# 1/rms of layer B's rows read from PSUM, their low parts on VectorE, and later weights' sums and scaling queued behind the rows

## Chip, cores and metric

The kernel runs on 1 core of one Trainium2 chip. The metric is the device time in microseconds (us) of one execution. The engines are TensorE (PE; its weight loads are PEld), VectorE (DVE), ScalarE (ACT), GpSimd (POOL) and SyncE (SP), which issues the DMAs. All engines work through their own queue in order.

## What is computed

A decoder trunk of two layers on 1024 tokens of width 1024. Layer A is a gated short convolution, layer B a stick-breaking attention with 16 heads of 64. What concerns the change is the seam between them: x1, the output of layer A, is normalised by its rms, and scaled and shifted with vectors worked out from c, before it is projected to keys, values, queries and the gate z.

```python
def rmsnorm(x, g):
    y = xf * lax.rsqrt(jnp.mean(xf * xf, axis=-1, keepdims=True) + EPS)
    return (y * g).astype(x.dtype)

def modulated_norm(x, g, shift, scale):
    return rmsnorm(x, g) * (1.0 + scale[:, None, :]) + shift[:, None, :]
...
# layer A ends with x1 = x + gate * (y @ w_out); then, for layer B:
hkv = modulated_norm(x, kv_norm_g, kv_shift, kv_scale)
k_flat, v_flat = jnp.split(hkv @ w_kv, 2, axis=-1)
h = modulated_norm(x, norm_g, shift, scale)
q, z = jnp.split(h @ w_qz, 2, axis=-1)
o = stick_breaking_attention(split_heads(q), k, v)
return x + gate * ((o * jax.nn.silu(z)) @ w_out)
```

## The kernel before

Activations lie transposed: the 1024 features are 8 tiles of 128 partitions (index kt or j), the 1024 tokens run along the free axis, cut into two halves of 512 columns. Each product of float32 numbers is made of three TensorE passes: both factors are split into a high part (a copy by ACT, rounded) and a low part (the difference), and high x high, high x low and low x high are summed in PSUM (lines 180 to 182 in `linear`). `split` makes the two parts: line 142 the high part on ACT, line 143 the low part on the engine that it is given. Weights go through the same `split` (whi, wlo), with POOL for the low part.

Layer B's gain is multiplied into the weights, not into the rows: `scaled` (line 158) multiplies a tile of weights by the gain, and `shift_terms` (lines 163 and 165: one start and seven sums on DVE) collects what the shift contributes; `shift_bias` makes a bias column of it. So the rows themselves need only 1/rms.

The stage of the change is the loop over the two halves near line 416. For each output tile j of layer A: weights are loaded and split, the row tile xr of xT is loaded into an s buffer (10 of them), TensorE sums 24 matmuls, DVE adds the gated result to xr (line 426, "the sum" in this text), SP writes it to x1_dram, ACT squares it (429, 432) and DVE adds up the squares (433). After eight tiles `rms_scale` sums the squares over features by transposing on TensorE and reducing on DVE (90, 91), works out 1/rms in twelve small DVE steps (197 to 204), broadcasts it to all partitions with four transpositions (210, "the row block"), and copies it from PSUM to an SBUF tile, rbc (217). DVE multiplies the eight rows by rbc (436), ACT makes x1h, and POOL makes x1l; in the second half every other x1l is made by DVE.

TensorE goes on with the second half's output tiles (s_3418 to s_3682 in the listings, j = 0 to 7) while the first half's rows are finished, and with keys and queries of the first half (`project_qkv(0)`) while the second half's are. Then come values, attention of head pair 0 (`attention`: scores L589 and L590, sigmoid L594, scan L598, transposition L608, the parts ah L611 and al L612, sums L622 and L623), the z projection of pair 0 (`silu_z`), and the projections of pair 1. Their weights come through `load_weights` with a gain, so `scaled` is called for each of them.

The order of each engine's queue is set when the program is built, by a scheduler that goes by its own estimate of the times; `tc.high_priority()` puts a block's instructions ahead where they could stand in several places. PSUM has four tags (mm, z, tr, o) of two banks each.

Of the kernel before, what the change touches and what calls it, by code (L numbers as in the profile page):

```python
# [9 lines left out]
F32 = mybir.dt.float32  # L10
F32R = mybir.dt.float32r
AF = mybir.ActivationFunctionType
ALU = mybir.AluOpType
AX = mybir.AxisListType.X

P = 128
D = 1024
T = 1024
KT = D // P
HALF = 512  # L20
# [17 lines left out]
def decoder_kernel(ctx, tc, vecs, xT, a_mod, kv_mod, b_mod, w_in, w_out_a, w_kv, w_qz, w_out_b, outT):  # L38
    nc = tc.nc
    PSUM = bass.MemoryType.PSUM  # L40

    const = ctx.enter_context(tc.tile_pool(name="const", bufs=1))
# [4 lines left out]

    PS_BUFS = {"mm": 2, "z": 2, "tr": 2, "o": 2}
    seq = [0]

    def ps_tile(tag):
        return psum.tile([P, HALF], F32, name=f"ps_{tag}", tag=tag, bufs=PS_BUFS[tag])

    def ps_any():
        tags = ("mm", "z", "tr")
        seq[0] += 1
        return ps_tile(tags[seq[0] % len(tags)])
# [36 lines left out]
    def column_sums(out, src):  # L94
        for _ in sum_groups(out, src):
            pass
# [44 lines left out]
    def split(hi, lo, full, lo_eng):  # L141
        nc.scalar.activation(hi, full, AF.Copy)  # L142
        lo_eng.tensor_tensor(lo, full, hi.bitcast(F32), op=ALU.subtract)  # L143


    def load_weights(src, gain=None, hi_tag="whi", lo_tag="wlo", pool=None, bufs=2, stage=None, shift=None):
        raw = (stage or raw_tile)()
        nc.sync.dma_start(raw, src)
        hi = (pool or wpool).tile([P, KT * P], F32R, name="whi", tag=hi_tag, bufs=bufs)
        lo = (pool or wpool).tile([P, KT * P], F32R, name="wlo", tag=lo_tag, bufs=bufs)  # L150
        terms = raw if gain is None else scaled(raw, gain, shift)
        split(hi, lo, raw, nc.gpsimd)
        return terms, hi, lo

    def scaled(raw, gain, shift):
        terms = shift_terms(raw, shift)
        raw3 = raw.rearrange("p (k n) -> p k n", k=KT)
        nc.vector.tensor_tensor(raw3, raw3, gain.unsqueeze(2).broadcast_to([P, KT, P]), op=ALU.mult)
        return terms

    def shift_terms(raw, shift):
        acc = const.tile([P, P], F32, name="bacc", tag="bacc", bufs=3)
        nc.vector.tensor_scalar(acc, raw[:, 0:P], shift[:, 0:1], None, op0=ALU.mult)
        for kt in range(1, KT):
            nc.vector.scalar_tensor_tensor(  # L165
                acc, raw[:, kt * P:(kt + 1) * P], shift[:, kt:kt + 1], acc, op0=ALU.mult, op1=ALU.add)
        return acc
# [17 lines left out]
    def rms_columns(ssq, lo_t=0, hi_t=T, more=None, total=None):  # L185
        n = (hi_t - lo_t) // P
        v = const.tile([P, 8], F32, name="rv", tag="rv", bufs=2)[:, :n]
        y = const.tile([P, 8], F32, name="ry", tag="ry", bufs=2)[:, :n]
        t = const.tile([P, 8], F32, name="rt", tag="rt", bufs=2)[:, :n]
        if total is not None:  # L190
            pass
        elif more is None:
            column_sums(v, ssq[:, lo_t:hi_t])
            total = v
        else:
            total = column_totals([(ssq[:, lo_t:hi_t], one), (more, one)], n)
        nc.vector.tensor_scalar(v, total, 1.0 / D, EPS, op0=ALU.mult, op1=ALU.add)
        I32 = mybir.dt.int32
        nc.vector.tensor_scalar(t.bitcast(I32), v.bitcast(I32), 1, None, op0=ALU.arith_shift_right)
        nc.vector.tensor_scalar(y.bitcast(I32), t.bitcast(I32), -1.0, float(0x5F3759DF), op0=ALU.mult, op1=ALU.add)  # L200
        for _ in range(3):
            nc.vector.tensor_mul(t, y, y)
            nc.vector.scalar_tensor_tensor(t, t, -0.5, v, op0=ALU.mult, op1=ALU.mult)
            nc.vector.scalar_tensor_tensor(y, t, 1.5, y, op0=ALU.add, op1=ALU.mult)
        return y

    def row_block(y, c0, w):
        pb = ps_tile("o")
        for i in range(w):
            nc.tensor.transpose(pb[:, i * P:(i + 1) * P], y[:, c0 + i:c0 + i + 1].broadcast_to([P, P]), ident)  # L210
        return pb[:, :w * P]
# [7 lines left out]
    def rms_scale(ssq, rbc, lo_t=0, hi_t=T):  # L219
        rms_rows(rms_columns(ssq, lo_t, hi_t), rbc, lo_t, hi_t)  # L220

    def halves():
        return [slice(h * HALF, (h + 1) * HALF) for h in range(NH)]
# [4 lines left out]
    tmp = papw.enter_context(tc.tile_pool(name="tmpa", bufs=1))  # L228

    def stile():  # L230
        return tmp.tile([P, HALF], F32, name="s", tag="s", bufs=10)

    rbc_a = const.tile([P, T], F32, name="rbc", tag="rbc", bufs=1)
    def ytile():
# [94 lines left out]
    with tc.high_priority():  # L329
        for sl in halves():  # L330
            for kt in range(KT):
                x = stile()
# [37 lines left out]
    for j in range(KT):  # L370
# [37 lines left out]
        if 2 <= j < 2 + len(PARTS):  # L408
            name, w, part, bcol, gcol = PARTS[j - 2]
            mods[name] = mod_vec(w, part, bcol, name, gain_col=gcol)  # L410


    rbc_b = const.tile([P, T], F32, name="rbc", tag="rbc", bufs=1)
    x1h = [xk.tile([P, T], F32R, name="x1h", tag="xk") for _ in range(KT)]
    x1l = [xk.tile([P, T], F32R, name="x1l", tag="xk") for _ in range(KT)]
    for sl in halves():
        ssq1 = tmp.tile([P, HALF], F32, name="ssq1", tag="graw", bufs=3)
        xs = []
        for j in range(KT):
            w = load_weights(w_out_a[j])[1:]  # L420
            xr = stile()
            xs.append(xr)
            nc.sync.dma_start(xr, xT[j * P:(j + 1) * P, sl])
            ps = ps_any()
            linear(ps, w, yh, yl, sl)
            nc.vector.scalar_tensor_tensor(xr, ps, mods["gate_a"][:, j:j + 1], xr, op0=ALU.mult, op1=ALU.add)
            nc.sync.dma_start(x1_dram[j, :, sl], xr)
            if j == 0:
                nc.scalar.activation(ssq1, xr, AF.Square)
            else:  # L430
                sq = tmp.tile([P, HALF], F32, name="sq1", tag="graw", bufs=3)
                nc.scalar.activation(sq, xr, AF.Square)
                nc.vector.tensor_add(ssq1, ssq1, sq)
        rms_scale(ssq1, rbc_b[:, sl], 0, HALF)
        for kt, x in enumerate(xs):
            nc.vector.tensor_mul(x, x, rbc_b[:, sl])
            split(x1h[kt][:, sl], x1l[kt][:, sl], x, nc.vector if sl.start and kt % 2 else nc.gpsimd)
        if sl.start == 0:

            def first_raw(raw, w, m):  # L440
                nc.sync.dma_start(raw, w)
                return raw, scaled(raw, mods["gain_" + m], mods["shift_" + m])

            firsts = [
                first_raw(tmp.tile([P, D], F32, name="raw1", tag="gacc", bufs=1), w_kv[0], "kv"),
                first_raw(tmp.tile([P, 2 + T], F32, name="raw1", tag="v", bufs=2)[:, :T], w_qz[0], "b"),
                first_raw(raw_tile(), w_kv[NPAIR], "kv")]
# [299 lines left out]
    for c, (a, b) in enumerate(CHUNKS):  # L747
        sl = slice(a, b)
        for j in range(EARLY, KT):
# [4 lines left out]
            sq = squares(j, sl, c == len(CHUNKS) - 1 and j == KT - 1)  # L754
# [45 lines left out]
```

## Time and profile before

| | us |
|---|---|
| median of 3 runs (lowest, highest) | 1213.46 (1213.27, 1217.39) |
| the profiled execution | 1214.38 |
| its span in the trace, first to last instruction | 1212.6 |
| PE busy | 1162.2 (96%) |
| PEld busy | 983.3 (81%) |
| DVE busy | 883.2 (73%) |
| ACT busy | 456.9 (38%) |
| POOL busy | 369.3 (30%) |

[...] Matmuls overlap, so one of 512 columns shows a duration of 0.39 us and starts every 0.23 us at the full clock; at half of it 0.63 and 0.43. Rows of the timeline give start and duration in us, engine, line, operation, output tile and inputs, the shape, the count of like instructions that are merged in the row, and in square brackets how long the engine sat idle before it and what ended that.

### The profile page before, as it was taken

To read this page: it belongs to the slowest core of one execution; us is meant where nothing else is said; L and a number is where in the kernel's file an instruction comes from. 1 tells how busy PE (TensorE), PEld (TensorE's weight loads), DVE (VectorE), ACT (ScalarE), POOL (GpSimd) and SP (SyncE) were. 2 spreads that over 40 slices of the span, in tenths; PEclk is the share of its full clock that TensorE was granted. 3 is DMA by queue.
4 is the path that set the end of the run, shared out by engine and by line. 5 is a ranking of instruction groups with operands and counts; after the bars stand their busy time and mean duration, and the time that the engine had idled before them with its cause. 6 is when DMAs were issued, how large, how long until landed. Compare 5 with 4: busy or idle time off the path is not lost.

```text
span 1212.6 us, 15743 instructions
## 1 busy us (share of the span) xinstructions
PE 1162.2 (96%) x5920; PEld 983.3 (81%) x5920; DVE 883.2 (73%) x1297; ACT 456.9 (38%) x750; POOL 369.3 (30%) x217
## 2 busy tenths in 40 slices
PE   7996999999999999879999999999999999999995
PEld 6884888888888888658888888888888888887885
DVE  7589841355445478676989888889988889677466
ACT  4324322111211233323455454454445445454341
POOL 3020544333423546532031231312223031221324
PEclk9797999999999999879999999999999999999997
DMA  9454431154354543413422313232232322553103
GB/s 373 175 167 147 159 101 52 51 175 147 119 182 151 168 139 137 148 39 91 101 66 61 105 53 83 66 89 77 68 84 72 94 68 61 156 206 125 56 16 138
DMA packets 61435, 138.45 MB, mean 114 GB/s; under 512 B 7472, under 2 KB 11696, under 8 KB 61360
## 3 DMA queue, kind: packets, MB, share of 16 engines
q1 hardware_dynamic: 61360, 137.46, 35.7%
q8 instruction: 46, 0.75, 0.3%
q14 instruction: 29, 0.24, 0.1%
HBM read 103.87 MB, written 14.68 MB: 98 GB/s over the span
## 4 chain that ended last, share of the span: by engine, by line
PE 78%; DVE 16%; issue 3%; ACT 1%; POOL 1%; DMA 1%; DVEq 0%; SPq 0%; POOLq 0%; ACTq 0%
PE ps_mm L180 11%; PE ps_mm L181 11%; PE ps_mm L182 11%; PE ps_tr L180 5%; PE ps_tr L181 5%; PE ps_tr L182 5%; PE ps_z L181 5%; PE ps_z L182 4%; PE ps_z L180 4%; PE ps_tr L608 4%; DVE sfx L598 4%; DVE bacc L165 3%; PE ps_o L623 3%; PE ps_o L622 2%; PE ps_z L590 2%
## 5 line engine op out<-in xcount | busy, mean ns | idle before, releaser
L143 POOL TENSOR_TENSOR wlo<-raw,whi 128x1024 fp32r<-128x1024 f32 x87 | 218.7, 2516 | 612.5 <-ACT whi L142 513.8
L598 DVE TENSOR_TENSOR_SCAN sfx<-sfx,floor 128x128 f32<-128x128 f32 (+2 forms) x192 | 221.1, 1171 | 17.2 <-ACT sfx L594 17.2
L181 PE MATMUL ps_mm<-x1l,whi 128*128 128x512 f32 x480 | 190.5, 397 | 4.4 <-DVE x1l L143 3.9
L180 PE MATMUL ps_mm<-x1h,whi 128*128 128x512 f32 x480 | 192.1, 400 | 2.6 <-ACT x1h L142 2.2
L182 PE MATMUL ps_mm<-x1h,wlo 128*128 128x512 f32 x480 | 188.5, 393 | 0.0
L142 ACT ACTIVATE whi<-raw 128x1024 fp32r<-128x1024 f32 x87 | 92.1, 1058 | 166.0 <-issue 60.1
L611 ACT ACTIVATE ah<-ps_tr,minus 128x512 fp32r<-128x512 f32 (+1 forms) x160 | 100.3, 645 | 108.2 <-PE ps_tr L608 106.7
L612 DVE SCALAR_TENSOR_TENSOR al<-ps_tr,ah 128x512 fp32r<-128x512 f32 (+1 forms) x160 | 97.3, 623 | 42.7 <-ACT ah L611 42.2
L594 ACT ACTIVATE sfx<-ps_z 128x128 f32<-128x128 f32 (+2 forms) x192 | 90.6, 491 | 81.6 <-PE ps_z L590 80.6
L181 PEld LDWEIGHTS ps_mm<-x1l,whi 128*128 128x128 f32 x480 | 90.8, 189 | 22.0 <-DVE x1l L143 4.6
L180 PEld LDWEIGHTS ps_mm<-x1h,whi 128*128 128x128 f32 x480 | 90.7, 189 | 20.6 <-ACT x1h L142 2.4
L182 PEld LDWEIGHTS ps_mm<-x1h,wlo 128*128 128x128 f32 x480 | 90.8, 189 | 17.7
L120 DVE SCALAR_TENSOR_TENSOR gacc<-graw,cs,gacc 128x512 f32<-128x512 f32 x84 | 71.2, 863 | 37.2 <-DMA graw<-b_mod 23.5
L623 PE MATMUL ps_o<-al,vv 128*128 128x256 f32 x320 | 83.2, 295 | 5.1 <-DVE al L612 5.0
L608 PE MATMUL ps_tr<-ident,sfx 128*128 128x128 f32 x576 | 87.2, 274 | 0.0
L622 PE MATMUL ps_o<-ah,vv 128*128 128x256 f32 x320 | 85.7, 281 | 0.1
L623 PEld LDWEIGHTS ps_o<-al,vv 128*128 128x128 f32 x320 | 60.4, 189 | 13.3 <-DVE al L612 10.1
L589 PE MATMUL ps_z<-kh,qq 128*128 128x128 f32 (+1 forms) x192 | 69.1, 365 | 0.7 <-ACT sfx L594 0.7
L622 PEld LDWEIGHTS ps_o<-ah,vv 128*128 128x128 f32 x320 | 60.5, 189 | 7.4 <-ACT ah L611 0.6
L608 PEld LDWEIGHTS ps_tr<-ident,sfx 128*128 128x128 f32 x576 | 65.4, 141 | 1.0
L590 PE MATMUL ps_z<-kl,qq 128*128 128x128 f32 (+1 forms) x192 | 65.4, 349 | 0.0
L181 PE MATMUL ps_mm<-nl,whi 128*128 128x512 f32 x152 | 59.8, 393 | 2.7 <-DVE nl L324 2.7
(280 smaller groups left out, 2482.2 us busy)
## 6 DMA issues: line engine op xcount, KB each, us to landing
raw<-w_in SPq DMA_DIRECT2D x29, 512.0 KB, 3.9
graw<-b_mod SPq DMA_DIRECT2D x48, 256.0 KB, 3.1
stage<-a_mod SPq DMA_DIRECT2D x16, 512.0 KB, 8.7
s<-xT SPq DMA_DIRECT2D x32, 256.0 KB, 4.5
graw<-kv_mod SPq DMA_DIRECT2D x32, 256.0 KB, 3.3
raw<-w_qz SPq DMA_DIRECT2D x16, 512.0 KB, 4.0
raw<-w_out_a SPq DMA_DIRECT2D x16, 512.0 KB, 3.6
raw<-w_kv SPq DMA_DIRECT2D x16, 512.0 KB, 3.6
```

Of the source, the lines that this page charges most:

```text
L142: nc.scalar.activation(hi, full, AF.Copy)
L143: lo_eng.tensor_tensor(lo, full, hi.bitcast(F32), op=ALU.subtract)
L180: nc.tensor.matmul(ps, lhsT=wh, rhs=ah[kt][:, sl], start=(kt == kts[0]), stop=False)
L181: nc.tensor.matmul(ps, lhsT=wh, rhs=al[kt][:, sl], start=False, stop=False)
L182: nc.tensor.matmul(ps, lhsT=wl, rhs=ah[kt][:, sl], start=False, stop=(kt == kts[-1]))
L594: nc.scalar.activation(om, zps[:, :w], AF.Sigmoid, scale=-SC)
L598: nc.vector.tensor_tensor_scan(rev, rev, floor[:, z0:z0 + w][:, ::-1], sf[r][:, s0 + w:s0 + w + 1], op0=ALU.mult, op1=ALU.max)
L608: nc.tensor.transpose(tp[:, s * P:(s + 1) * P], rows[r][:, jb * P - c0:(jb + 1) * P - c0], ident)
L611: nc.scalar.activation(ah[:, :w], tp[:, :w], AF.Identity, bias=minus)
L612: nc.vector.scalar_tensor_tensor(al[:, :w], tp[:, :w], -1.0, ah[:, :w].bitcast(F32), op0=ALU.add, op1=ALU.subtract)
L622: nc.tensor.matmul(ops[:, cols], lhsT=vs, rhs=ah[:, rs], start=first, stop=False)
L623: nc.tensor.matmul(ops[:, cols], lhsT=vs, rhs=al[:, rs], start=False, stop=end)
```

## The change

The column sums of the squares are made by matmuls with one column (a path that `rms_columns` had, and the kernel's last chunk used): the running sum of seven squares and the eighth square go in apart, so the last addition on DVE and the reduce fall away. 1/rms is not copied to SBUF: the multiplications read the row block in PSUM. All low parts x1l are made by DVE. The block stands under `tc.high_priority()`. Weights with a gain call `scaled` under `tc.issue_after(...)`: in the order these instructions stand behind the last x1l made so far; for pair 0's z weights and all later ones that is the last row of the second half. The s buffers become 11.

```diff
@@ load_weights @@
-        terms = raw if gain is None else scaled(raw, gain, shift)
+        if gain is None:
+            terms = raw
+        else:
+            with tc.issue_after(last["x1"].ins):
+                terms = scaled(raw, gain, shift)
         split(hi, lo, raw, nc.gpsimd)
@@ stile @@
-        return tmp.tile([P, HALF], F32, name="s", tag="s", bufs=10)
+        return tmp.tile([P, HALF], F32, name="s", tag="s", bufs=11)
@@ the loop over halves @@
-    rbc_b = const.tile([P, T], F32, name="rbc", tag="rbc", bufs=1)
...
                 nc.scalar.activation(sq, xr, AF.Square)
-                nc.vector.tensor_add(ssq1, ssq1, sq)
-        rms_scale(ssq1, rbc_b[:, sl], 0, HALF)
-        for kt, x in enumerate(xs):
-            nc.vector.tensor_mul(x, x, rbc_b[:, sl])
-            split(x1h[kt][:, sl], x1l[kt][:, sl], x, nc.vector if sl.start and kt % 2 else nc.gpsimd)
+                if j < KT - 1:
+                    nc.vector.tensor_add(ssq1, ssq1, sq)
+        with tc.high_priority():
+
+            scale = row_block(rms_columns(ssq1, 0, HALF, sq), 0, 4)
+            for kt, x in enumerate(xs):
+                nc.vector.tensor_mul(x, x, scale)
+                nc.scalar.activation(x1h[kt][:, sl], x, AF.Copy)
+                last["x1"] = nc.vector.tensor_tensor(x1l[kt][:, sl], x, x1h[kt][:, sl].bitcast(F32), op=ALU.subtract)
```

Three places of the queues. In the listings of the changed kernel lines are 4 to 8 higher: the sum is L430, the addition of squares L438, the multiplication L443, x1l on DVE L445, `scaled` L163, `shift_terms` L168 and L170.

DVE, the first half's rows, between the sums of the second half's tiles j=1 and j=2; before:

```order
L426 SCALAR_TENSOR_TENSOR s<-ps_tr,gate_a,s 128x512
L433 TENSOR_TENSOR ssq_3411<-ssq_3411,sq_3483 128x512
L217 COPY rbc<-ps_o 128x512
L436 TENSOR_TENSOR s<-s,rbc 128x512 x8
L426 SCALAR_TENSOR_TENSOR s<-ps_mm,gate_a,s 128x512
```

DVE at the same place in the changed kernel:

```order
L430 SCALAR_TENSOR_TENSOR s<-ps_tr,gate_a,s 128x512
L443 TENSOR_TENSOR s<-s,ps_o 128x512 x8
L438 TENSOR_TENSOR ssq_3411<-ssq_3411,sq_3483 128x512
L445 TENSOR_TENSOR x1l<-s,x1h 128x512 x5
L430 SCALAR_TENSOR_TENSOR s<-ps_mm,gate_a,s 128x512
L445 TENSOR_TENSOR x1l<-s,x1h 128x512 x3
L430 SCALAR_TENSOR_TENSOR s<-ps_z,gate_a,s 128x512
```

The copy is gone, and five low parts stand ahead of the sum of j=2 and three more ahead of that of j=3. The low part of tile 0, which frees the buffer that j=3's row is loaded to, was POOL's before.

TensorE, where the second half's tile j=5 (ps_mm_3608, weights whi_3602) begins; before:

```order
L180 MATMUL ps_mm_3608<-yh_664,whi_3602 128x512
L181 MATMUL ps_mm_3608<-yl_665,whi_3602 128x512
L180 MATMUL ps_z_3646<-yh_664,whi_3640 128x512
L181 MATMUL ps_z_3646<-yl_665,whi_3640 128x512
L182 MATMUL ps_mm_3608<-yh_664,wlo_3603 128x512
L180 MATMUL ps_mm_3608<-yh_820,whi_3602 128x512
```

And in the changed kernel:

```order
L185 MATMUL ps_mm_3608<-yh_664,whi_3602 128x512
L186 MATMUL ps_mm_3608<-yl_665,whi_3602 128x512
L187 MATMUL ps_mm_3608<-yh_664,wlo_3603 128x512
L185 MATMUL ps_mm_3608<-yh_820,whi_3602 128x512
L186 MATMUL ps_mm_3608<-yl_821,whi_3602 128x512
```

The two matmuls of tile j=6 (ps_z_3646) now stand behind the whole of j=5. In the same queue the row block of the first half stands 12 matmuls earlier than before, behind two matmuls of j=2; that of the second half stands where it stood, behind the first half's queries, with the totals' one-column matmuls after 22 of the 48 matmuls of the first half's keys and queries.

DVE, the second half's 1/rms, from the last sum on; before (the start):

```order
L426 SCALAR_TENSOR_TENSOR s<-ps_tr,gate_a,s 128x512
L173 TENSOR_REDUCE bias<-ps_mm 128x1
L163 TENSOR_SCALAR bacc<-raw,shift_b 128x128
L165 SCALAR_TENSOR_TENSOR bacc<-raw,shift_b,bacc 128x128
L433 TENSOR_TENSOR ssq_3411<-ssq_3411,sq_3711 128x512
L165 SCALAR_TENSOR_TENSOR bacc<-raw,shift_b,bacc 128x128 x6
L158 TENSOR_TENSOR raw<-raw,gain_b 128x1024
L173 TENSOR_REDUCE bias<-ps_mm 128x1
L163 TENSOR_SCALAR bacc<-raw,shift_kv 128x128
L91 TENSOR_REDUCE rv<-ps_o 128x4
```

And in the changed kernel the end of the same stretch:

```order
L209 SCALAR_TENSOR_TENSOR ry<-rt,ry 128x4
L178 TENSOR_REDUCE bias<-ps_mm 128x1
L443 TENSOR_TENSOR s<-s,ps_o 128x512 x8
L178 TENSOR_REDUCE bias<-ps_mm 128x1
L445 TENSOR_TENSOR x1l<-s,x1h 128x512 x8
L168 TENSOR_SCALAR bacc<-raw,shift_b 128x128
L168 TENSOR_SCALAR bacc<-raw,shift_kv 128x128
```

The sums and scalings of two weights (bacc and raw) have moved from among the steps of 1/rms to behind the last low part, where they are dealt between the evacuations of keys and queries. The x1h of a row waits for its multiplication alone, each x1l for all eight.

## Rows read from the trace of the kernel before

**Rows 1.** Windows: us; PE, PEld, DVE, ACT, POOL busy; PEclk; DMA share; GB/s.

```profile
485.50:495.70 10.20, 4.81 (x12) 3.43 (x12) 6.63 (x6) 4.83 (x7) 9.87 (x6) 0.67 0.76 241
495.70:509.60 13.90, 13.90 (x62) 11.46 (x61) 6.44 (x5) 3.39 (x4) 4.82 (x2) 1.00 0.35 126
521.50:540.10 18.60, 9.97 (x25) 6.83 (x26) 17.66 (x27) 7.03 (x11) 9.42 (x6) 0.63 0.07 15
```

**Rows 2.** Timeline of TensorE, first hole: tile j=5 (ps_mm) and j=6 (ps_z).

```profile
487.80 0.50 PE L180 MATMUL ps_mm<-yh,whi 128*128 128x512 f32 x1 [2.20 <-ACT whi L142]
...
491.73 0.79 PE L180 MATMUL ps_z<-yh,whi 128*128 128x512 f32 x1 [3.20 <-ACT whi L142]
```

**Rows 3.** Timeline of ACT in the first hole.

```profile
485.65 0.63 ACT L432 ACTIVATE sq<-s 128x512 f32<-128x512 f32 x1 [3.45 <-DVE s L426]
...
486.71 1.04 ACT L142 ACTIVATE whi<-raw 128x1024 fp32r<-128x1024 f32 x1
...
490.64 1.04 ACT L142 ACTIVATE whi<-raw 128x1024 fp32r<-128x1024 f32 x1
```

**Rows 4.** Timeline of DVE ahead of the first hole.

```profile
473.40 11.56 DVE L436 TENSOR_TENSOR s<-s,rbc 128x512 f32<-128x512 f32 x8
484.88 0.74 DVE L426 SCALAR_TENSOR_TENSOR s<-ps_mm,gate_a,s 128x512 f32<-128x512 f32 x1
```

**Rows 5.** Timeline of POOL, same stretch.

```profile
479.23 9.81 POOL L143 TENSOR_TENSOR x1l<-s,x1h 128x512 fp32r<-128x512 f32 x6
489.00 2.35 POOL L143 TENSOR_TENSOR wlo<-raw,whi 128x1024 fp32r<-128x1024 f32 x1
```

**Rows 6.** Timeline of DVE, from the stage's last sum to the second half's rows.

```profile
509.86 0.75 DVE L426 SCALAR_TENSOR_TENSOR s<-ps_tr,gate_a,s 128x512 f32<-128x512 f32 x1 [1.55 <-PE ps_tr L182]
...
517.85 0.69 DVE L91 TENSOR_REDUCE rv<-ps_o 128x4 f32<-128x512 f32 x1
...
521.21 1.23 DVE L158 TENSOR_TENSOR raw<-raw,gain_kv 128x1024 f32<-128x1024 f32 x1
...
524.90 8.18 DVE L436 TENSOR_TENSOR s<-s,rbc 128x512 f32<-128x512 f32 x8
```

**Rows 7.** Timeline of TensorE, second hole and the z projection of pair 0.

```profile
521.22 0.27 PE L172 MATMUL ps_mm<-ident,bacc 128*128 128x128 f32 x1
523.51 0.62 PE L210 MATMUL ps_o<-ident,ry 128*128 128x128 f32 x4 [2.02 <-DVE ry L204]
526.31 0.71 PE L180 MATMUL ps_mm<-x1h,whi 128*128 128x512 f32 x1 [2.17 <-ACT x1h L142]
...
534.81 0.80 PE L181 MATMUL ps_mm<-x1l,whi 128*128 128x512 f32 x1 [3.90 <-DVE x1l L143]
...
552.20 0.45 PE L180 MATMUL ps_mm<-x1h,whi 128*128 128x512 f32 x1
```

**Rows 8.** Groups by line and shape, DVE, 440 to 545 us: count, busy us, mean ns.

```profile
L436 DVE TENSOR_TENSOR s<-s,rbc 128x512 f32<-128x512 f32 x16 | 19.7, 1304 | 0.1
...
L143 DVE TENSOR_TENSOR x1l<-s,x1h 128x512 fp32r<-128x512 f32 x4 | 5.8, 1502 | 0.0
...
L165 DVE SCALAR_TENSOR_TENSOR bacc<-raw,shift_kv,bacc 128x128 f32<-128x128 f32 x14 | 4.9, 351 | 0.2
```

**Rows 9.** The same view from 70 to 545 us: layer A's multiplications by 1/rms.

```profile
L353 DVE TENSOR_TENSOR s<-s,rbc 128x512 f32<-128x512 f32 x4 | 2.7, 685 | 0.0
...
L353 DVE TENSOR_TENSOR s<-ps_tr,rbc 128x512 f32<-128x512 f32 x2 | 1.4, 678 | 0.0
```

**Rows 10.** Timeline of DVE, end of the kernel: 1/rms of the last 256 columns.

```profile
1202.31 0.16 DVE L197 TENSOR_SCALAR rv<-ps_o 128x2 f32<-128x2 f32 x1 [1.55 <-PE ps_o L104]
...
1206.30 2.74 DVE L743 TENSOR_TENSOR out<-x,ps_o 128x256 f32<-128x256 f32 x8 [0.84 <-PE ps_o L210]
```

**Rows 11.** The page's DMA issues: KB each, median us to landing.

```profile
s<-xT SPq DMA_DIRECT2D x32, 256.0 KB, 4.5
```

**Rows 12.** The page's costliest groups: the scan of the attention.

```profile
L598 DVE TENSOR_TENSOR_SCAN sfx<-sfx,floor 128x128 f32<-128x128 f32 (+2 forms) x192 | 221.1, 1171 | 17.2 <-ACT sfx L594 17.2
```

More of the change, by code (lines that the diff above doesn't have):

```diff
@@ L49, in decoder_kernel @@
     seq = [0]
+    last = {}
     def ps_tile(tag):
```

## The prediction

> **What bounds the kernel now.** I read the windows of the stage around the change first, since the share of busy time over the whole span (TensorE 96%) hides where TensorE is not fed. Between 462 and 560 us there are two holes [rows 1]: from 485.5 to 495.7 TensorE works 4.81 of 10.2 us at a granted clock of 0.67, and from 521.5 to 540.1 it works 9.97 of 18.6 us at 0.63. Between them it is never idle (13.90 of 13.90). So an edit here pays only by what it takes out of these two holes, and whatever VectorE (DVE) saves elsewhere is worth nothing.
>
> *First hole.* TensorE's own rows name what it waits for: 2.20 us, then 3.20 us, each for a ScalarE (ACT) copy of weights, whi [rows 2]. ACT's rows show why these are late: the first copy, at 486.71, stands behind the square that starts at 485.65, and the second, at 490.64, again behind a square [rows 3]. A square waits for its sum on DVE (L426), and the sum of tile j=2, at 484.88, stands behind eight multiplications of rows by 1/rms that take 11.56 us [rows 4]. GpSimd (POOL) is late too: six low parts x1l in one piece until 489.0, and only then the low part of the same weights, which ends at 491.35 [rows 5]; the third matmul of tile j=5 needs it. The next sum (j=3) waited for its xT tile, whose buffer such a low part frees.
>
> *Second hole.* DVE's rows: the last sum of the stage starts at 509.86 (A below), but the reduce that begins 1/rms starts at 517.85, since shift sums and scalings of later weights are dealt in between (the one at 521.21 is 1.23 us, ahead of steps that the chain still needs); then the copy of 1/rms to SBUF, and at 524.90 the multiplications, 8.18 [rows 6]. TensorE finishes its cover at 521.49, waits 2.02 us for the last step of 1/rms, 2.17 for the first x1h, and 3.90 for a low part that DVE writes only after all eight multiplications [rows 7].
>
> **The change part by part.**
>
> *Multiplications read PSUM.* The 16 of before have two SBUF inputs and take 1304 ns in the mean [rows 8]. The nearest rows with a PSUM input and the same 512 columns are L353's: 678 ns, and 685 where both inputs are in SBUF and none was stopped [rows 9]. So the place of the operand costs nothing by itself; what falls away is the waiting for POOL. I take 0.61 us from start to start (L743, 8 of 256 columns in 2.74 us [rows 10], is 0.34 each, the same plus its fixed part): 4.9 us for eight. The two copies go. L353's two rows put PSUM 7 ns lower, so I charge nothing for it. [...]
>
> *Low parts on DVE.* 16 instead of 4; POOL loses 12. DVE's four took 1502 ns in the mean [rows 8]. Alone they should take what L353's SBUF form takes, 685 ns [rows 9], 0.61 start to start. Low bound 0.61, high 1.50. In the first half POOL now has only one weights' part per 5.4 us of TensorE (2.35 us each [rows 5]), so DVE is stopped once, not eight times: I take 0.61 and one stop of 2.4 us per half.
>
> *First hole, worked.* 1/rms is sent out on TensorE 12 matmuls earlier (its place in the queue, told with the change), some 2.7 us at 0.224 us a matmul (13.90 us for 62 [rows 1]), and the copy is gone, so the rows start near 470.3 instead of 473.4. Eight at 0.61 end at 475.2; one square's addition; five low parts with one stop for POOL's 2.4 us: 481.2; the sum of j=2 then, against 484.88. Its square ends by 482.6, the weights' copy of j=5 (1.04 us as in [rows 3]) by 483.7, its low part on POOL, whose x1l are gone, by 486.2. TensorE reaches j=5 at 485.5 plus 0.5 for the eight one-column matmuls that replace four transpositions, and its third matmul 0.45 later: no wait, or one below 0.3 us. The two matmuls of j=6 that stood third and fourth in j=5's block, and waited for the second copy, have moved behind it. The load of j=3's row is issued when the first low part is done (about 479) and lands 4.5 later [rows 11], ahead of its sum. So the 24.1 us from 485.5 to 509.6 shrink to 74 matmuls (12 and 62 in the windows) at 0.224 = 16.6: 7.5 less 0.5, **7.0 us**. Low bound: low parts at 1.50 each put the sum of j=2 at 484.9 as before, TensorE again waits 2.2 us and POOL's gain alone is left, 2 us. High bound 7.5.
>
> *Second hole, worked, from A.* TensorE's 48 matmuls of cover end at A+11.6 plus 0.5 for the added ones, and the row block now follows in its queue without waiting, if 1/rms is ready. The same chain at the kernel's end takes 3.99 us from totals to the first PSUM multiplication [rows 10]; the totals stand 22 matmuls into the cover, near A+6, so it is ready at A+10, with the later weights' steps out of its way. The queue of TensorE, not DVE, decides: multiplications at A+12.9 (before A+15.0). They end at A+17.8; the first low part, behind one small reduce, at A+18.6, and TensorE runs from A+18.7 without a stop. Before, it ran from 534.81, A+24.95, with eight of the half's 48 matmuls done, in the changed queue two: 6 more, 1.36 us at the full clock. I leave the slow stretch after resuming as long as it was (534.8 to 540.1), as TensorE is idle about as long. 24.95 - 18.7 - 1.36 = **4.9 us**. With low parts at 1.50 DVE still feeds TensorE, which takes six matmuls per low part, only the first is 0.9 later: low bound 4.0; high 5.5 with a shorter slow stretch.
>
> *Later weights' sums and scaling behind the rows.* Two sets: 14 sums at 351 ns [rows 8], two starts, two scalings at 1.23 [rows 6], some 8 us. They lay in front of the rows; now they follow the last low part (A+25.1), dealt among the evacuations of keys and queries, and the first set ends near A+32. Cover: the z projection of head pair 0, at 552.20 (A+42.3) [rows 7], 4.9 earlier A+37.4. Its weights need 1.04 on ACT [rows 3] and 2.4 on POOL after the scaling: A+35.5. Cost nothing, margin 1.9 us; past it each microsecond counts fully.
>
> *Square sums by one-column matmuls, an 11th s buffer.* The last addition and two reduces fall off DVE, in the cover. The extra buffer moves one xT load and with it DVE's order near 84 to 112 us, where DVE is full. Following the rows there, TensorE has three matmuls more behind it at the same time: a gain of 0.7, or a loss of as much; I take 0.
>
> **Sum.** 7.0 + 4.9 = 11.9 us from the profiled execution's 1214.38: 1202.5. The median shown lies 0.9 below that execution; between the two I say **1202**.
>
> **Rivals.**
>
> *A, the low parts on DVE are stopped by POOL throughout.* A DVE operation with two SBUF inputs takes 1304 to 1502 ns where POOL works beside it, and 685 where it was not stopped [rows 8, 9]; the low parts keep two SBUF inputs. If each takes 1.50, the first hole gives 2 and the second 4: 1208.4. For it: the four of before ran beside a single weights' part and still took 1502. Against: that mean holds one long stop, and POOL's queue is nearly empty now. [...]
>
> *B, nothing to speak of: the order of the first two head pairs gives it back.* The order of DVE and TensorE differs through head pairs 0 and 1 as well, where DVE is nearly full. If the attention there loses 6 to 10 us, 1209 to 1213. For it: a long list of swaps of scans and al. Against: many put al earlier, which is what TensorE waits for.
>
> *C, slower.* The same mechanism with a larger price: an al behind a scan, 1171 ns [rows 12], stops TensorE. The gain is used up when ten of the some 40 al of two pairs are so delayed, and the kernel is slower by over 0.5% from 16 on (18 us): 1221 at 16.
>
> **How the numbers follow.** Forecast (both holes shrink, gain 9 to 14): 0.66. A: 0.16, of which about half is still over 0.5%. B: 0.12. C: 0.06. 0.5% is 6.1 us, about what a measurement of this kernel can tell from none. Faster 0.66 + 0.08 + a little of B = 0.78; same 0.16; slower 0.06. The range takes the high bounds (7.5 + 5.5 + 0.7, so 1200) with a microsecond over, and on the other side A: 1199 to 1209, leaving out B's far half and C.
>
> **What would show it.** Right: multiplications at 0.6 to 0.75 us each; TensorE's wait for whi before j=5 below 0.5 us and its clock at full until the second hole; the second hole's row block without a wait; one wait of about 4 us for x1h and x1l; no wait for the z weights of pair 0; POOL without x1l. Wrong: a low part over 1 us in the mean, a wait for wlo of j=5, al waits in pairs 0 and 1, or a longer slow stretch in the second hole.

## The result, and the profile after

The changed kernel takes 1199.51 us in the median (1197.34 to 1202.63) against 1214.26 for the kernel before, measured beside it: a ratio of 0.9887, 95% interval 0.9857 to 0.9918. Forecast were 1202, 1199 to 1209. Run a second time (`changed_again` below) it took 1201.68, a ratio of 0.9901 (0.9875 to 0.9927).

The windows of the changed kernel, with the columns of [rows 1]:

```profile
460.00:480.00 20.00, 20.00 (x94) 16.63 (x94) 17.98 (x31) 10.06 (x15) 7.79 (x3) 1.00 0.41 135
480.00:500.00 20.00, 20.00 (x90) 16.51 (x89) 13.85 (x12) 6.50 (x9) 9.61 (x4) 1.00 0.57 183
...
512.50:521.50 9.00, 4.62 (x15) 3.11 (x14) 8.60 (x15) 6.91 (x11) 1.29 (x1) 0.81 0.01 2
```

The first hole is gone: TensorE is busy without a break at the full clock (1.00) from 460 to 500 (and on to 512.5: 12.50 of 12.50 us, at 1.00). Of the second, 9 us are left, in which it works 4.62.

DVE of the changed kernel, where [rows 4] and [rows 6] show the kernel before:

```profile
467.55 4.87 DVE L443 TENSOR_TENSOR s<-s,ps_o 128x512 f32<-128x512 f32 x8
...
472.95 5.29 DVE L445 TENSOR_TENSOR x1l<-s,x1h 128x512 fp32r<-128x512 f32 x5
478.16 0.74 DVE L430 SCALAR_TENSOR_TENSOR s<-ps_mm,gate_a,s 128x512 f32<-128x512 f32 x1
478.82 1.88 DVE L445 TENSOR_TENSOR x1l<-s,x1h 128x512 fp32r<-128x512 f32 x3
...
508.76 0.16 DVE L209 SCALAR_TENSOR_TENSOR ry<-rt,ry 128x4 f32<-128x4 f32 x1
512.76 0.29 DVE L178 TENSOR_REDUCE bias<-ps_mm 128x1 f32<-128x128 f32 x1 [3.83 <-PE ps_mm L177]
513.19 4.87 DVE L443 TENSOR_TENSOR s<-s,ps_o 128x512 f32<-128x512 f32 x8
517.98 0.28 DVE L178 TENSOR_REDUCE bias<-ps_mm 128x1 f32<-128x128 f32 x1
518.18 7.11 DVE L445 TENSOR_TENSOR x1l<-s,x1h 128x512 fp32r<-128x512 f32 x8
```

Eight multiplications take 4.87 us, not 11.56 and 8.18. The low parts take 5.29 and 1.88 in the first half, 7.11 in the second. The last step of 1/rms is at 508.76, and DVE then sits idle for 3.83 us until TensorE comes to the bias and the row block, which stand next to each other in its queue.

ACT and POOL of the changed kernel, the two parts of the weights of j=5:

```profile
479.47 1.05 ACT L143 ACTIVATE whi<-raw 128x1024 fp32r<-128x1024 f32 x1
```

```profile
480.59 2.41 POOL L144 TENSOR_TENSOR wlo<-raw,whi 128x1024 fp32r<-128x1024 f32 x1 [4.11 <-ACT whi L143]
```

TensorE of the changed kernel at the second hole, for [rows 7]; the first row is one of the two batches of one-column matmuls that make the totals:

```profile
505.59 0.95 PE L105 MATMUL ps_o<-one,sq 128*128 128x1 f32 x8
...
512.55 0.60 PE L215 MATMUL ps_o<-ident,ry 128*128 128x128 f32 x4
...
514.60 0.50 PE L185 MATMUL ps_z<-x1h,whi 128*128 128x512 f32 x1 [1.17 <-ACT x1h L444]
...
518.32 0.80 PE L185 MATMUL ps_mm<-x1h,whi 128*128 128x512 f32 x1 [3.22 <-DVE bias L178]
518.92 0.80 PE L186 MATMUL ps_mm<-x1l,whi 128*128 128x512 f32 x1
```

The row block no longer waits. The long wait that is left is put down to a bias: the reduce at 517.98 stands behind the eight multiplications and holds a PSUM bank that the keys need. The first x1l, at 518.18, comes 0.2 us later still, and the matmul that takes it starts at 518.92 without a wait of its own; mending the bias alone would have gained little.

**Where the time went.** Three rows cut the span into stretches that can be compared between runs: the transposition of gacc on TensorE near 235 us (gacc is transposed several times; this one makes shift_kv), the stage's last sum on DVE (A), and the last gating product on POOL (G). Of the kernel before, A being in [rows 6]:

```profile
235.20 1.03 PE L90 MATMUL ps_o<-ident,gacc 128*128 128x128 f32 x8
...
1130.30 1.29 POOL L644 TENSOR_TENSOR o<-o,sgb 128x512 f32<-128x512 f32 x1
```

Of the changed kernel's second profile, `changed_again`:

```profile
233.86 1.03 PE L91 MATMUL ps_o<-ident,gacc 128*128 128x128 f32 x8
...
502.06 0.75 DVE L430 SCALAR_TENSOR_TENSOR s<-ps_tr,gate_a,s 128x512 f32<-128x512 f32 x1 [1.48 <-PE ps_tr L187]
...
1117.10 1.29 POOL L652 TENSOR_TENSOR o<-o,sgb 128x512 f32<-128x512 f32 x1
```

The differences of such rows, for all kernels of this study (us, one profile each; the median is that of all runs):

| kernel | to gacc | gacc to A | A to G | G to end | median |
|---|---|---|---|---|---|
| before | 235.20 | 274.66 | 620.44 | 82.3 | 1214.26 |
| changed | 231.59 | 268.18 | 613.45 | 82.4 | 1199.51 |
| changed_again | 233.86 | 268.20 | 615.04 | 82.4 | 1201.68 |
| s_buffers_10 | 230.24 | 268.20 | 615.41 | 82.6 | 1199.73 |
| no_deferral | 234.92 | 268.20 | 615.64 | 82.5 | 1200.32 |
| xl_on_pool | 231.67 | 270.90 | 615.55 | 82.6 | 1203.24 |
| rbc_in_sbuf | 228.55 | 269.61 | 615.83 | 82.5 | 1202.91 |
| before_11_buffers | 235.85 | 273.04 | 620.53 | 82.4 | 1210.91 |
| psum_operand_alone | 235.28 | 273.47 | 614.48 | 82.6 | 1207.22 |
| interleaved_second_half | 236.56 | 268.20 | 613.92 | 82.5 | 1200.76 |
| early_row_block_alone | 227.29 | 268.20 | 613.21 | 82.4 | 1197.17 |
| early_row_block | 232.07 | 268.20 | 610.39 | 82.5 | 1194.21 |
| early_and_z_first | 231.50 | 268.20 | 609.74 | 82.3 | 1194.65 |

Between the two profiles of the changed kernel the first stretch differs by 2.3 us and A to G by 1.6, nothing else: 3.9 of the 3.9 us between their spans. So the change is worth 6.5 us from gacc to A (the first hole) and 5.4 to 7.0 from A to G (the second hole and the attention behind it), 11.9 to 13.5 in all; the medians of the two comparisons say 14.75 and 10.6. What its first profile gained ahead of gacc is scatter: up to that row `s_buffers_10` has the order of the kernel before, and reaches it at 230.24 against 235.20, while `before_11_buffers` has that of the changed kernel, at 235.85 against 231.59.

### The profile page after: what moved, and what is told of

Same layout as the page of the kernel before. It is cut to its first block, busy times and chain, and to the rows that moved or that the text cites. A ratio compares the mean times of both kernels' runs of the same rounds, so it can differ in the third digit from the quotient of the medians.

```text
span 1195.6 us, 15782 instructions
## 1 busy us (share of the span) xinstructions
PE 1156.4 (97%) x5944; PEld 980.7 (82%) x5944; DVE 868.5 (73%) x1303; ACT 456.9 (38%) x750; POOL 351.9 (29%) x205
## 4 chain that ended last, share of the span: by engine, by line
PE 82%; DVE 13%; issue 2%; ACT 1%; DMA 1%; POOL 0%; DVEq 0%; SPq 0%; ACTq 0%; POOLq 0%
PE ps_mm L185 12%; PE ps_mm L186 12%; PE ps_mm L187 12%; PE ps_z L187 5%; PE ps_z L186 5%; PE ps_tr L186 5%; PE ps_tr L187 5%; PE ps_tr L185 5%; PE ps_z L185 5%; PE ps_tr L616 4%; DVE sfx L606 3%; PE ps_o L631 3%; PE ps_o L630 2%; PE ps_z L598 2%; PE ps_z L597 2%
## 5 line engine op out<-in xcount | busy, mean ns | idle before, releaser
L606 DVE TENSOR_TENSOR_SCAN sfx<-sfx,floor 128x128 f32<-128x128 f32 (+2 forms) x192 | 226.1, 1198 | 17.5 <-ACT sfx L602 17.5
L185 PE MATMUL ps_z<-nh,whi 128*128 128x512 f32 x152 | 60.3, 397 | 2.2 <-ACT nh L328 2.2
```

The source lines that it names most:

```text
L185: nc.tensor.matmul(ps, lhsT=wh, rhs=ah[kt][:, sl], start=(kt == kts[0]), stop=False)
L606: nc.vector.tensor_tensor_scan(rev, rev, floor[:, z0:z0 + w][:, ::-1], sf[r][:, s0 + w:s0 + w + 1], op0=ALU.mult, op1=ALU.max)
```

## The experiments

The first four take one part out of the changed kernel.

**Low parts back on POOL.** `xl_on_pool`:

```diff
-last["x1"] = nc.vector.tensor_tensor(x1l[kt][:, sl], x, ...)
+last["x1"] = (nc.vector if sl.start and kt % 2 else nc.gpsimd).tensor_tensor(x1l[kt][:, sl], x, ...)
```

> The changed kernel with the low parts x1l where they were before (all of the first half and four of the second on POOL), so POOL works beside the multiplications again. Theory 1 (the prediction's): a multiplication with a PSUM operand isn't stopped by POOL, so it keeps 0.60 to 0.75 us in the mean; POOL's x1l start some 4 us earlier than in the kernel before, so wlo of j=5 is late by 1 us at most, and in the second half POOL makes x1l of row 0 while DVE still multiplies: 1198.5 to 1201. Theory 2 (the gain in the first hole came from POOL's emptied queue): wlo of j=5 stands behind six x1l and TensorE waits 2 us and more for it again, with the clock at half for some us after it: 1202 to 1205. Theory 3 (POOL stops a multiplication whatever its operand): 1.2 to 1.3 us each, the sum of j=2 is back behind 10 us of them, both holes come back: 1207 to 1210.

Measured: 1203.24, ratio 0.9916 (0.9887 to 0.9944). POOL at the first half's rows in this kernel:

```profile
467.72 2.42 POOL L144 TENSOR_TENSOR wlo<-raw,whi 128x1024 fp32r<-128x1024 f32 x1 [3.08 <-ACT whi L143]
470.11 8.52 POOL L445 TENSOR_TENSOR x1l<-s,x1h 128x512 fp32r<-128x512 f32 x6
478.59 2.35 POOL L144 TENSOR_TENSOR wlo<-raw,whi 128x1024 fp32r<-128x1024 f32 x1
```

DVE and TensorE, same kernel:

```profile
467.65 4.87 DVE L443 TENSOR_TENSOR s<-s,ps_o 128x512 f32<-128x512 f32 x8
```

```profile
481.00 0.50 PE L187 MATMUL ps_tr<-yh,wlo 128*128 128x512 f32 x1 [1.22 <-POOL wlo L144]
```

POOL works through the whole time of the multiplications, and they take 4.87 us all the same: theory 3 is out, these multiplications with a PSUM operand are not stopped. But wlo stands behind six x1l again and TensorE waits for it, so 2.7 us of the first hole come back. The mechanism and the time are theory 2's; the waits, 1.22 us here and one of 0.52 for a whi before it, are shorter than its 2 us, and from 481.33 on matmuls again start every 0.23 us, the spacing of the full clock.

**1/rms in SBUF again.** `rbc_in_sbuf`:

```diff
-scale = row_block(rms_columns(ssq1, 0, HALF, sq), 0, 4)
+rms_rows(rms_columns(ssq1, 0, HALF, sq), rbc_b[:, sl], 0, HALF)
+scale = rbc_b[:, sl]
```

> The changed kernel with 1/rms copied to SBUF again, so that the multiplications have two SBUF operands; the low parts stay on DVE and POOL's queue stays empty of them. Theory 1 (the operand's place keeps POOL's stops away): the multiplications are stopped now and then by the weights' parts, 0.85 to 1.0 us in the mean like the x1l of the changed kernel (956 ns); the first hole stays closed, the second grows by the copy and 8 times 0.25 us, 2.5 us in all: 1201 to 1203. Theory 2 (POOL's emptied queue is what made them fast): 0.68 to 0.72 us each, and only the copy of some 0.7 us is lost in the second hole: 1199.5 to 1200.5.

Measured: 1202.91, ratio 0.9915 (0.9885 to 0.9945). DVE, then POOL, at the first half's rows:

```profile
465.13 2.42 DVE L439 TENSOR_TENSOR ssq<-ssq,sq 128x512 f32<-128x512 f32 x1
467.47 4.89 DVE L445 TENSOR_TENSOR s<-s,rbc 128x512 f32<-128x512 f32 x8
```

```profile
464.59 2.41 POOL L144 TENSOR_TENSOR wlo<-raw,whi 128x1024 fp32r<-128x1024 f32 x1 [3.09 <-ACT whi L143]
471.65 7.57 POOL L144 TENSOR_TENSOR wlo<-raw,whi 128x1024 fp32r<-128x1024 f32 x2 [4.65 <-ACT whi L143]
```

The multiplications take 680 ns each, the figure of theory 2, but by chance of place: POOL was idle from 467.0 to 471.65. The addition ahead of them, with two SBUF inputs, took 2.42 instead of 0.68 until POOL's 2.41 were over. So this kernel does not show that an emptied POOL is enough. Its cost of 1.4 us from gacc to A lies where neither theory had it. TensorE of this kernel waits for the first of the two wlo:

```profile
476.48 0.50 PE L187 MATMUL ps_tr<-yh,wlo 128*128 128x512 f32 x1 [1.08 <-POOL wlo L144]
```

That one, beside DVE's instructions with two SBUF inputs, takes about 4.8 of the 7.57 us (it starts at 471.65, the matmul that needs it at 476.48), where the one above that meets only the addition takes 2.41: here the stopping went both ways. The time lies in theory 1's range, but theory 1 had the first hole closed and the multiplications slow. From A to G it is 0.8 and 2.4 us above the changed kernel's two profiles, which does not part the theories.

**No deferral.** `no_deferral`:

```diff
-with tc.issue_after(last["x1"].ins):
-    terms = scaled(raw, gain, shift)
+terms = scaled(raw, gain, shift)
```

> The changed kernel without the order that puts later weights' sums and scalings behind the rows: one set (start, seven sums, scaling, some 4 us) stands ahead of the second half's 1/rms again, and single sums stand among the low parts. Theory 1 (DVE has nothing else to do between the last sum and the totals, some 6 us, and the row block's place in TensorE's queue decides): the chain of 1/rms ends as early as with the deferral, the three sums among multiplications and low parts cost 0.3 us each: 1199.5 to 1201. Theory 2 (the prediction counted the deferral as part of the second hole's gain): TensorE waits for 1/rms before the row block, 2 us and more, 1202 to 1204.

Measured: 1200.32, ratio 0.9894 (0.9859 to 0.9928): theory 1. DVE and TensorE of this kernel, whose A is at 503.12:

```profile
504.30 4.70 DVE L169 SCALAR_TENSOR_TENSOR bacc<-raw,shift_b,bacc 128x128 f32<-128x128 f32 x7
509.09 1.23 DVE L162 TENSOR_TENSOR raw<-raw,gain_b 128x1024 f32<-128x1024 f32 x1
510.23 0.15 DVE L201 TENSOR_SCALAR rv<-ps_o 128x4 f32<-128x4 f32 x1
```

```profile
517.96 0.50 PE L184 MATMUL ps_z<-x1h,whi 128*128 128x512 f32 x1 [1.16 <-ACT x1h L443]
521.68 0.79 PE L184 MATMUL ps_mm<-x1h,whi 128*128 128x512 f32 x1 [3.22 <-DVE bias L177]
```

A whole set of sums and its scaling fit ahead of the totals; 1/rms begins at A+7.1 (A+6.8 in the changed kernel), and TensorE's two waits and their places, A+14.8 and A+18.6, are the same. The other set stands behind 1/rms here too, from 516.33 on, without having been told to. The deferral gained nothing that these runs resolve.

**Ten s buffers.** `s_buffers_10`, with `bufs=10` in `stile`, and the counterpart `before_11_buffers`, the kernel before with `bufs=11`:

> The changed kernel with ten s buffers as before. Theory 1 (the prediction: the extra buffer moves an xT load near 84 to 112 us and is worth 0, give or take 0.7 us): 1199 to 1200.5, and the profiled run still reaches the second stage some 3 us earlier than the kernel before. Theory 2 (the 3.6 us by which the profiled run of the changed kernel was ahead at 232 us came from the buffer): the time from 84 to 112 us is as in the kernel before, and the kernel takes 1202 to 1203.5.

> The kernel before with eleven s buffers and nothing else. Theory 1 (the prediction: 0, give or take 0.7 us): as the kernel before within 1 us, ratio 0.999 to 1.001. Theory 2 (the early stage's 3.6 us came from the buffer): 3 to 4 us faster, ratio 0.997.

Measured: 1199.73, ratio 0.9906 (0.987 to 0.9943), and 1210.91, ratio 0.9981 (0.996 to 1.0003). With ten buffers the changed kernel has the same 268.20 from gacc to A, and no later gacc: theory 1. In the kernel before, the eleventh is worth 1.6 us from gacc to A, since j=3's row no longer comes late (its sum had waited 1.36 us for the load); neither theory had this place. The interval of the ratio covers what both theories gave, but gacc does not come earlier with eleven buffers, as theory 2 needs.

**One part alone.** `psum_operand_alone` is the kernel before with only this:

```diff
-rms_scale(ssq1, rbc_b[:, sl], 0, HALF)
+scale = row_block(rms_columns(ssq1, 0, HALF), 0, 4)
 for kt, x in enumerate(xs):
-    nc.vector.tensor_mul(x, x, rbc_b[:, sl])
+    nc.vector.tensor_mul(x, x, scale)
```

> The kernel before with one part of the change alone: the multiplications read the row block in PSUM, and the two copies to SBUF go; POOL keeps its x1l, the sums by transposition and the order of later weights stay. Theory 1 (the operand's place keeps POOL's stops away): 0.60 to 0.75 us each instead of 1.30; the sum of j=2 comes 5 us earlier, which leaves 0 to 2 us of TensorE's 5.4 us of waits for whi, and the second hole shrinks by the copy and 8 times 0.4, 3 to 4 us: 1204 to 1208. Theory 2 (POOL stops them all the same): 1212 to 1213.

Measured: 1207.22, ratio 0.995 (0.9928 to 0.9971), in theory 1's range. DVE, POOL and TensorE at the first hole:

```profile
478.12 0.75 DVE L425 SCALAR_TENSOR_TENSOR s<-ps_mm,gate_a,s 128x512 f32<-128x512 f32 x1 [0.48 <-DMA s<-xT]
```

```profile
479.11 8.51 POOL L143 TENSOR_TENSOR x1l<-s,x1h 128x512 fp32r<-128x512 f32 x6
487.58 5.11 POOL L143 TENSOR_TENSOR wlo<-raw,whi 128x1024 fp32r<-128x1024 f32 x2
```

```profile
490.42 0.79 PE L182 MATMUL ps_mm<-yh,wlo 128*128 128x512 f32 x1 [3.01 <-POOL wlo L143]
```

The multiplications take 4.86 us for eight, and the sum of j=2 comes at 478.12 instead of 484.88, yet only 1.2 of the 6.5 us are gained up to A: whi's wait became a wait of 3.01 for wlo, behind POOL's x1l. From A to G, however, this edit alone gives 6.0, as much as the whole change. Theory 1 is right on the multiplications, but it had 3 to 4 us for the second hole and as much or more for the first: that the time lies in its range is luck, two errors that cancel.

The next three go on from the changed kernel, to what is left of the second hole.

**Interleaving.** `interleaved_second_half`:

```diff
+low = []
 for kt, x in enumerate(xs):
-    nc.vector.tensor_mul(x, x, scale)
+    if kt > 1 and sl.start:
+        with tc.issue_after(low[kt - 2].ins):
+            nc.vector.tensor_mul(x, x, scale)
+    else:
+        nc.vector.tensor_mul(x, x, scale)
...
+    low.append(nc.vector.tensor_tensor(x1l[kt][:, sl], x, ...))
```

> The changed kernel with DVE's order in the second half written out: from the third row on, a multiplication stands behind the low part of the row two before it, so x1l of row 0 follows after two multiplications instead of eight. Theory 1 (what is left of the second hole is the 4 us in which TensorE has the first x1h but no x1l, and a bias that stands behind eight multiplications): TensorE goes on 3 to 4 us earlier, takes six matmuls (1.36 us) per row while DVE needs 1.3 to 1.5 for a row's two instructions, and is held back little: 1196 to 1198. Theory 2 (ACT's x1h comes too late for the alternation, so each row costs DVE a wait of 0.5 us, and TensorE runs in pieces at the half clock): 1199 to 1201.

**The row block earlier.** `early_row_block` adds this for the first half's queries (`linear` was given two arguments for where a sum begins and ends); `early_row_block_alone` is the changed kernel with this and without the interleaving:

```diff
+linear(ps, qw[:2], x1h, x1l, sl, range(4), False)
+with tc.issue_after(last["rb"].ins):
+    linear(ps, qw[:2], x1h, x1l, sl, range(4, KT), True, False)
```

> The interleaved kernel, with the second half's row block also moved ahead of the last 12 matmuls of the first half's queries (2.7 us at the full clock); in the changed kernel 1/rms was ready 3.8 us before TensorE sent it out. Theory 1 (TensorE's queue decides when the rows start): the 12 matmuls cover the first two multiplications, x1h and x1l of row 0, TensorE hardly waits, a wait of 0.5 us at most, and another 1.5 to 2.7 us are saved against the interleaved kernel: 1193.5 to 1196. Theory 2 (1/rms isn't ready at the earlier place, or the clock's slow stretch comes anyway): TensorE waits at the row block instead, and the time is that of the interleaved kernel within 0.7 us.

> The changed kernel with the second half's row block moved ahead of 12 matmuls of the first half's queries, and nothing else; the eight multiplications still stand ahead of the low parts. Theory 1 (the 12 matmuls, 2.7 us, fill time in which TensorE waited; it still has no x1l until eight multiplications are through, 5.6 us after the row block): TensorE waits 2 to 3 us instead of 4.4, and goes on 2.7 us earlier than in the changed kernel, measured from the last sum; from the last sum to the end 693 to 694.5 us, median 1197 to 1198.5. Theory 2 (only both edits together close the hole; a wait of 2 us still brings the half clock, and the z weights come too late): 695 to 696.5 us, median 1199 to 1200.5.

Measured: 1200.76 (0.9897, 0.9865 to 0.9928), 1194.21 (0.9846, 0.9815 to 0.9878) and 1197.17 (0.9868, 0.9837 to 0.9899). TensorE's waits from A to the z projection of pair 0, in this order of kernels:

```profile
519.60 0.50 PE L185 MATMUL ps_z<-x1h,whi 128*128 128x512 f32 x1 [1.16 <-ACT x1h L449]
...
538.87 0.50 PE L185 MATMUL ps_mm<-x1h,whi 128*128 128x512 f32 x1 [2.31 <-ACT whi L143]
```

```profile
531.84 0.50 PE L185 MATMUL ps_mm<-x1h,whi 128*128 128x512 f32 x1 [1.62 <-ACT whi L143]
```

```profile
511.74 0.60 PE L186 MATMUL ps_z<-x1l,whi 128*128 128x512 f32 x1 [2.48 <-DVE x1l L445]
```

Interleaving closes the hole down to 1.16 us, as theory 1 said, and TensorE then runs into the z weights 2.31 us too early: their scaling stands behind the rows. A wait had only moved, and the time is that of the changed kernel, in theory 2's range by another mechanism than theory 2's. With the row block earlier as well, the hole is gone. The windows of `early_row_block`, the hole and then the z weights' wait:

```profile
510.30:521.50 11.20, 11.20 (x54) 9.27 (x53) 10.61 (x20) 6.01 (x10) 0.00 (x0) 1.00 0.01 1
528.20:540.00 11.80, 10.09 (x43) 7.42 (x42) 7.96 (x10) 3.96 (x7) 6.43 (x4) 1.00 0.86 192
```

TensorE never stops in the hole, and the wait of 1.62 leaves the clock at full. From A to G it gains 3.1 to 4.7 us on the changed kernel's two profiles. The early row block alone gains in the hole what theory 1 said: its wait is 2.48, and from A to the first matmul of pair 0's z projection it takes 34.35 us, against 36.54 and 38.00 in the changed kernel's two profiles. But from there to G it takes 578.86, against 576.91 and 577.04, so that A to G, 613.21, is at theory 2's end, though the median is theory 1's. TensorE's waits for al from 500 us on are 5.9 us in all against 4.3, which points at the order of head pairs 0 and 1; since `s_buffers_10` without this edit has 578.08, it stays open how much of the loss is the edit's.

**The z weights' set not deferred.** `early_and_z_first` is `early_row_block` with the first set of sums and scaling left undeferred:

```diff
+sets[0] += 1
+if sets[0] == 1:
+    terms = scaled(raw, gain, shift)
+else:
+    with tc.issue_after(last["x1"].ins):
+        terms = scaled(raw, gain, shift)
```

> The kernel with the early row block and the interleaved second half, with one set of sums and scaling not deferred: that of the z weights of head pair 0, which then lies in the 6 us that DVE has free between the last sum and the totals. Theory 1 (what was left were the 1.6 us for which TensorE waited for these weights, late because their scaling stood behind the rows): that wait goes, TensorE has no wait from the last sum to the attention, and from the last sum to the end it takes 1.5 to 2.5 us less than with the early row block alone (692.9 us): 690.5 to 691.5, median 1192 to 1193.5. Theory 2 (the wait only moves to the next weights, whose set is still behind the rows, or the set delays 1/rms): 692 to 694, median 1194 to 1195.

Measured: 1194.65, ratio 0.9855 (0.9828 to 0.9881). The wait for whi is gone; one of 0.69 for a key's high part came in its place:

```profile
525.30 0.47 PE L190 MATMUL ps_mm<-x1h,whi 128*128 128x512 f32 x1 [0.69 <-ACT kh L520]
```

A to the end takes 692.0 us instead of 692.9, the near end of theory 2's range, and the median is theory 2's: a wait moved once more. It and `early_row_block` beat both kernels, the latter by some 19 us against the kernel before (1213.25 beside it); the two cannot be told apart.

**The changed kernel again.** `changed_again`, no edit:

> The changed kernel once more, to have its times beside those of its variants on one chip. Theory 1 (the time of a kernel scatters by some 5 us from run to run through its first 120 us, after which its rows lie at fixed distances): from the last sum to the end 694.5 to 697.5 us again (695.8 in the first profile), wherever the run starts; median 1198.5 to 1201.5. Theory 2 (its first profile was a lucky one throughout): 698 us or more from the last sum to the end, median above 1202.

Measured: 1201.68, 697.4 us from A to the end. Theory 1, at its upper end, with the median 0.2 us above its range.

## Why the prediction was right, point by point

**First hole: 7.0 forecast, 6.5 measured.** The chain behind it came out step by step. Shifted by the 3.6 us by which this run reached gacc earlier, the rows start at 471.2 (forecast 470.3), the sum of j=2 at 481.8 (481.2), whi of j=5 ends at 484.1 (483.7), and wlo at 486.6 (486.2). TensorE had no wait at all. Two conditions were needed, faster rows and an emptied POOL, and the prediction had both: `psum_operand_alone` has the faster rows without the emptied POOL and gains 1.2, `xl_on_pool` has them and the earlier row block without it and gains 3.8. With 1/rms in SBUF but both conditions met, `rbc_in_sbuf` still gains 5.1. One term was mis-sized: for the one-column matmuls 0.5 us more was charged, but each of their two batches holds the next matmul back by 0.81 us (505.59 to 506.40), where the four transpositions took 0.35, so it was 1.3; other terms made up for a part of it. The low bound's 484.9 for the sum of j=2 does not follow from its terms, which give 483.4 (475.2, 0.7 and five times 1.50). What the earlier row block and the one-column sums are worth by themselves, no run shows.

**Multiplications and low parts.** 0.60 us from start to start (forecast 0.61). Eight low parts took 7.17 and 7.11 us, that is 4.9 and one POOL stop of 2.3 per half (forecast 2.4). Rival A needed them stopped throughout, 1.50 each; they took 956 ns in the mean. That POOL does not stop a multiplication with an input in PSUM was not shown by the multiplications that the prediction names: POOL was idle beside L353's (from 72.56 to 88.67 us and from 91.17 on) and L743's (from 1203.67 on). The runs show it: eight take 4.87 us in `xl_on_pool`, with POOL at work throughout, and 4.86 in `psum_operand_alone`, with POOL at work from the third on, and the addition with two SBUF inputs in `rbc_in_sbuf` takes 2.42 us instead of 0.68.

**PSUM operand at no extra cost.** 680 ns with one input in PSUM (changed kernel), 680 ns with both in SBUF (`rbc_in_sbuf`); eight take 4.87 and 4.89 us.

**Second hole: 4.9 forecast, 4.3 and 5.8 measured, the size right, part of the reason wrong.** From A to the first matmul of pair 0's z projection, with the same 120 matmuls of 512 columns before it, the kernel before takes 42.34 us, the changed kernel 38.00 and 36.54 in its two profiles. The rest of the 5.4 and 7.0 from A to G lies behind this row. TensorE runs on from A+18.55, but with an x1h; the first x1l matmul, which the forecast had at A+18.7, is at A+19.15, late by the one-column matmuls again. The forecast left the slow stretch after resuming as long as it had been, 5.3 us; it lasted 6.2 in `changed_again` and 3.1 in the first profile after the same wait (both are shown at the end); that the forecast fell between them was luck. The step that failed is the one that set "the later weights' steps out of its way" as a condition of the early 1/rms: `no_deferral` has 1/rms just as early for TensorE with one set ahead of it, and `psum_operand_alone`, with the old order and TensorE still waiting 2.05 us for 1/rms, gains 6.0. So the PSUM operand and the missing copy are enough for a gain of this size. Why the rest of the change adds nothing here is shown only in part: in `psum_operand_alone` POOL makes low parts while DVE multiplies, and TensorE has its first x1l matmul at A+17.1, two us earlier than with all low parts on DVE; but `xl_on_pool`, with POOL's low parts and the changed kernel's row block, still waits 1.39 us for the bias and takes 36.97 to the z projection. Not foreseen either: the bias behind the eight multiplications.

**Deferral at no cost, margin 1.9 us.** No cost, but the margin was 0.8: the z projection at 536.31 stands 0.8 us behind the end of its wlo, at 535.50. What the prediction said of the time past it, that each microsecond counts fully, is what `interleaved_second_half` then showed.

**Early stage at 0.** Right. **Rivals B and C.** The attention gave nothing back: from the z projection of pair 0 to G the changed kernel takes 577.04 and 576.91 us, the kernel before 578.10. In `early_row_block_alone` an effect of B's kind may show, of up to 2 us.

**The sum.** 11.9 us were forecast, and the stretches give 11.9 and 13.5. The medians, 14.75 and 10.6 us less than the kernel before, lie on both sides of it by the scatter of the first 120 us and of the clock; that the first of them, 1199.51, still fell half a microsecond inside the range owes something to luck.

## What to carry to other kernels

When one engine feeds a stage through two others, look at both queues: making the rows fast only turned a wait for whi into one for wlo, until POOL's queue was emptied too. A hole that is filled makes the next weights due earlier, so work that was deferred at no cost must be priced again, and the free time ahead of the hole is where it belongs. Compare stretches between fixed rows of two profiles: here gacc to A agrees to 0.02 us in the two profiles of one kernel, and A to G, with the clock's hole in it, to 1.6, where whole runs of one kernel scatter by 5 and more.

## What the runs showed of the hardware that was not expected

The first 120 us differ from run to run. The same windows of the changed kernel, first profile:

```profile
20.00:40.00 20.00, 20.00 (x115) 17.53 (x116) 15.18 (x18) 10.35 (x11) 2.85 (x1) 0.91 1.03 418
...
100.00:120.00 20.00, 18.86 (x73) 14.74 (x72) 19.95 (x39) 7.45 (x12) 0.00 (x0) 0.88 0.31 103
```

Second profile:

```profile
20.00:40.00 20.00, 19.98 (x107) 17.36 (x108) 13.98 (x17) 8.25 (x9) 2.86 (x1) 0.83 1.03 418
...
100.00:120.00 20.00, 17.29 (x64) 13.43 (x64) 20.00 (x37) 8.61 (x13) 0.00 (x0) 0.83 0.36 117
```

TensorE's granted clock there is 0.91 and 0.88 in the one, 0.83 and 0.83 in the other, with 115 and 107 matmuls done in the first window. Over all kernels of the table gacc comes between 227.3 and 236.6 us.

The clock's answer to one and the same hole differs too. After the wait of 3.22 us, at the same distance from A, the changed kernel's two profiles show:

```profile
518.17:519.77 1.60, 1.45 (x3) 1.04 (x4) 1.60 (x4) 1.60 (x3) 0.00 (x0) 0.50 0.00 0
519.77:521.77 2.00, 2.00 (x7) 1.53 (x7) 2.00 (x3) 1.05 (x2) 1.56 (x1) 0.60 0.15 34
```

```profile
520.46:522.06 1.60, 1.44 (x3) 1.03 (x4) 1.60 (x4) 1.60 (x3) 0.00 (x0) 0.50 0.00 0
522.06:524.06 2.00, 2.00 (x6) 1.52 (x6) 2.00 (x3) 1.07 (x2) 1.55 (x1) 0.50 0.15 33
524.06:526.06 2.00, 2.00 (x6) 1.53 (x5) 2.00 (x2) 0.00 (x0) 1.18 (x1) 0.50 0.45 98
526.06:528.06 2.00, 2.00 (x9) 1.64 (x8) 2.00 (x11) 0.00 (x0) 0.00 (x0) 0.82 0.00 0
```

By the granted clock half rate ended near 521.4 in the one (0.60 is 1.6 of 2.00 us at 0.50) and near 526.8 in the other (0.82 is 0.7 of 2.00 us at 0.50), 3.1 and 6.2 us after the resumption, with identical rows before. In the first profile matmuls start every 0.43 us at half rate and every 0.23 behind it, so of 3.1 us more at half rate about half is lost, close to the 1.6 us between their stretches from A to G. It sets how closely a hole's price can be forecast.
